# A decoder layer's MLP on Trainium2: conversions and a half block of matmuls issued ahead of other work

## The chip, the cores and the metric

The kernel runs on one core of a Trainium2 chip as a single launch. The metric is the device time of one execution in microseconds. TensorE (PE) does the matrix products, VectorE (DVE), ScalarE (ACT) and GpSimd (POOL) the element-wise work, and SyncE (SP) issues the DMAs. Each engine takes its own instructions in the order in which the program issues them, and engines wait for each other through semaphores; so the order in which the Python program emits instructions is the order within each engine.

## The reference

The reference is one inference step of one decoder layer in float32. It has 512 prompt tokens and 8 samples of 8 tokens, 576 tokens in all, with width 1024. Attention in three dilated groups and a gated linear recurrence run side by side, are gated and merged, projected, added to the input and normalised. The change lies in what follows:

```python
x1 = _layer_norm(DN_ALPHA * x + g1 * mix, ln1_g, ln1_b, dtype)
u2 = x1 * (1 + sc2) + sh2
hid = jnp.square(jax.nn.relu(jnp.einsum('bsd,df->bsf', u2, w_up) + b_up))
ff = jnp.einsum('bsf,fd->bsd', hid, w_down) + b_down
x2 = _layer_norm(DN_ALPHA * x1 + g2 * ff, ln2_g, ln2_b, dtype)
```

The hidden width is 4096. The outputs are both groups' activations, the new caches and the recurrent states.

## The kernel before, in words

**Precision.** Every large product is made of three float32r products. A float32 operand is split into a high part (ACT's copy to float32r: `whi`, `hdh`, `u2h`) and the rest (a subtraction, nearly always on DVE: `wlo`, `hdl`, `u2l`). Then high by high, low by high and high by low are added up in one PSUM bank. So each weight tile costs one ACT and one DVE instruction before PE can use it.

**Weights** come in units of 512 columns, each loaded by SP in two slots of four K tiles (1 MB each). There are three raw buffers (`NRAW = 3`). `load_more` issues the next load when a buffer has been given back by `weights_done`, which is called when the last conversion out of a slot has been issued; the DMA itself then waits for that conversion.

**Order.** The program's main line emits PE's blocks one by one. Side work (the layer norm, transposes, row copies) stands in generators; `side.pump`, called after every few matmuls, advances them by a planner's costs and due times, and `side.drain` runs them out.

**The MLP, from 940 us on.** Tokens are worked on in two halves of 288 (`HF`). The layer norm of half 1 (`layer_norm_1(1)`) runs as side work while the first unit (`mlp[0]`, blocks n = 0 to 3 of the hidden layer, 128 columns each) does half 0. Each half block is 24 matmuls (8 K tiles by 3). `split_once` converts the unit's blocks ahead, the last of them at n = 1. Within the norm, PE sums squares (`sx<-sq`), ACT copies the sum (`lns`), PE spreads it (`sx<-lns`), ACT takes the root and DVE the reciprocal (`lnr`); then come, for each of the 8 K tiles, `u2t`, `u2h` and `u2l`. After `side.drain()` the four blocks of half 1 run interleaved by K tile over four PSUM banks, so that each K tile is used by all four as soon as it is there; then the four evacuations follow (bias and ReLU, square, `hdh`, `hdl`).

After that comes the list `seq` of steps. A `Plain` step is one block of 128 output columns, done as two halves `pe(0)` and `pe(1)`, each followed by its evacuation `ev`. It starts with the second unit (`mlp[1]`, blocks 4 to 7 of the hidden layer) and the first eight blocks of the down product. The other three quarters have up units made of seven block products each (`Seventh`, f = 0 to 6, a Strassen-like scheme with sums of weight blocks and of inputs), two units of 512 columns to a quarter, followed by eight down blocks (`Plain`; only the first two of these three quarters have them in `seq`). The step methods are `sum` (DVE, sums of weight blocks), `cast` (ACT, high part), `low` (DVE, low part), `pe`, `ev`, `fin` (ACT, square and high part of the hidden layer) and `sub` (DVE, its low part). `lag` says how many steps ahead `sum` and `cast` are issued. The loop at the end of the listing writes the order out by hand. Weights of these steps lie in the pool `parts` (6 buffers), which takes the memory of the pools `small` and `caches` that the front part used; `front.close()` gives those back.

**The end.** The last quarter's down product is made in three units `ud[0]`, `ud[1]`, `ud[2]`. `blocks` does the tokens from 256 on, as before with hidden channels on the partitions, and `tokens_major` turns the result by PE transposes (bank `tr`) that ACT and DVE copy out. `tiles` does the first 256 tokens, with tokens on the partitions: per tile of 128 tokens 24 matmuls of 512 columns. The order is `blocks(ud[0])`, `blocks(ud[1])`, `tiles(ud[1])`, `tiles(ud[2])`. `ud[1]` is converted during the fourth block of `ud[0]` (`pass_on`), `ud[2]` during the two tiles of `ud[1]`: K tiles 0 to 3 with the subtraction on POOL, 4 to 7 with it on DVE. `add_up` multiplies a finished tile by the gate (`gps`), adds it to the residual (`res`) and takes statistics (`st`); `normalize` ends the second layer norm with DVE and POOL instructions on `res` and stores the result.

Of the kernel before, what the change touches and what calls it, by code (L numbers as in the profile page):

```python
# [14 lines left out]
AF = mybir.ActivationFunctionType  # L15
# [4 lines left out]
KT = D // 128  # L20
# [5 lines left out]
HF = NT // 2  # L26
# [25 lines left out]
NPG = 62  # L52
NKV = 6
NWP = 6
AHEAD_K = 8
LN2 = 2500
SPH = 0
NRAW = 3
KV_AHEAD = 4
QB_AHEAD = 4  # L60
# [185 lines left out]
def decoder_step(ctx, tc, I, O):  # L246
# [24 lines left out]
    def bank(shape, tag, bufs=2):  # L271
        return psum.tile(shape, F32, name=tag, tag=tag, bufs=bufs)
# [54 lines left out]
    def load_more(force=False):  # L327

        while leaving and (force or leaving[0] <= side.now):
            leaving.popleft()  # L330
        while load_q and live[0] + len(leaving) < NRAW:
            load_one()
# [26 lines left out]
        if j == len(u["blocks"]) - 1:  # L359
            weights_done(u["slots"])  # L360

    def split_k(u, k, eng=V):

        if k in u["w"]:
            return
        load_more(True)
        t = u["slots"][k // 4][2][:, k % 4]
        w = u["w"][k] = page([128, 512], "whi", F32R), page([128, 512], "wlo", F32R)
        A.activation(w[0], t, AF.Copy)
        eng.tensor_sub(w[1], t, w[0])  # L370
        if k % 4 == 3:
            weights_done(u["slots"][k // 4:k // 4 + 1])

    def split_once(u, j):
        if j not in u.setdefault("split", set()):
            u["split"].add(j)
            split(u, j)
# [11 lines left out]
    def mm_part(w, nk, xs, h, ps, ks):  # L389
        hi, lo = w  # L390
        seq = [(hi, 0), (hi, 1), (lo, 0)]
        n = 0
        for k in ks:
            for m, (ww, xi) in enumerate(seq):
                PE.matmul(ps, ww[k // 4][:, k % 4], xs[xi][k][:, h * HF:(h + 1) * HF],
                          start=(k == 0 and m == 0), stop=(k == nk - 1 and m == 2))
                n += 1
                if n % 8 == 0 and n < 3 * len(ks):
                    side.pump(8 * 123.0)
# [1387 lines left out]
    def half(u, j, xs, h, evac):  # L1787
        ps = bank([128, HF], "lin")
        mm_half(u["w"][j], 8, xs, h, ps)
        evac(h, ps)  # L1790
        side.pump(8 * 123.0)
# [3 lines left out]

    u = mlp[0]
    ups = [up_evac(0, n, True) for n in range(4)]
    for n in range(4):
        for m in range(n + 1, min(n + 3, 4)):
            split_once(u, m)  # L1800
        half(u, n, U2, 0, ups[n])
    side.drain()
    banks = [bank([128, HF], "lin" if n < 2 else "att") for n in range(4)]
    for k in range(KT):
        for n in range(4):
            mm_part(u["w"][n], 8, U2, 1, banks[n], (k,))
    for n in range(4):
        ups[n](1, banks[n])
        u["w"].pop(n)

    def down_evac(qd, n):
        def evac(hf, ps):
            if qd == 0:
# [52 lines left out]
    def wpart(shape, name):  # L1866
        return parts["pool"].tile(shape, F32R, name=name, tag="part")
# [16 lines left out]
    class Plain(Step):  # L1884
# [2 lines left out]

        def __init__(self, u, j, xs, evac, order=((0, range(KT)), (1, range(KT)))):
            self.u, self.j, self.xs, self.evac, self.order = u, j, xs, evac, order

        def src(self):
            return [t[:, :, self.j * 128:(self.j + 1) * 128] for _, _, t in self.u["slots"]]
# [16 lines left out]
        def pe(self, i):  # L1909
            h, ks = self.order[i]  # L1910
            self.ps = ps = getattr(self, "ps", {})
            ps[i] = bank([128, HF], "lin")
            for k in ks:
                for m, (w, xi) in enumerate(((self.hi, 0), (self.hi, 1), (self.lo, 0))):
                    PE.matmul(ps[i], w[:, k], hv(self.xs[xi][k], h), start=(k == ks[0] and m == 0),
                              stop=(k == ks[-1] and m == 2))
                if k == ks[3]:
                    side.pump(12 * 133.0)
            side.pump(12 * 133.0)
# [24 lines left out]
    class Seventh(Step):  # L1944


        def __init__(self, unit, f):
            self.U, self.f = unit, f
            self.lag = 2 if f in (1, 2) else 3

        def sum(self):
            f, b = self.f, self.U.blk
# [86 lines left out]
    for qd in range(4):  # L2039
        for n in range(8):  # L2040
            if qd == 0 and n < 4:
                continue
            if qd == 0:
                seq.append(Plain(mlp[1], n % 4, U2, up_evac(0, n)))
            elif n % 4 == 0:
                unit_ = Unit(mlp[qd * 4 + n // 4], qd, n)
                seq += [Seventh(unit_, f) for f in range(7)]
        if qd < 3:
            for n in range(8):

                order = {} if qd == 0 or n else {"order": ((1, (0, 1, 2, 3, 6, 7, 4, 5)), (0, range(KT)))}
                seq.append(Plain(mlp[qd * 4 + 2 + n // 4], n % 4, (Hd[0], Hd[1]), down_evac(qd, n), **order))
# [35 lines left out]
                yield 436, None  # L2088
        gate.append(True)

    front.close()
    parts["pool"] = ctx.enter_context(tc.tile_pool(name="parts", bufs=NWP))
    n_down = len(seq) - 22

    def at(i, what, *a):
        if 0 <= i < len(seq):
            getattr(seq[i], what)(*a)

    at(0, "cast")
    at(0, "low")  # L2100
    for i, st in enumerate(seq):
        if i < 4:
            for k in (2 * i, 2 * i + 1):
                for h in range(2):
                    G.tensor_mul(hv(hT[k], h), hv(hT[k], h), rstds[h])
        if i == 4:
            side.add("p", input_sums())
        if i == 12:
            side.drain()
        if n_down <= i < n_down + 8:  # L2110
            if i == n_down:
                side.flush(True)
                reload(0)
            if i < n_down + 7:
                reload(i - n_down + 1)
        at(i - 1, "ev", 1)
        if i + 1 < len(seq) and seq[i + 1].lag == 1:
            at(i + 1, "cast")
        at(i + 1, "low")
        if i + 2 < len(seq) and seq[i + 2].lag > 2:  # L2120
            at(i + 2, "cast")
        if i and isinstance(st, Plain) and isinstance(seq[i - 1], Seventh):
            for n in (1, 2):
                at(i - n, "fin" if n == 1 else "sub")
            at(i - 1, "sub")
        st.pe(0)
        st.ev(0)
        if not isinstance(st, Plain):
            at(i - 1, "fin")
            at(i - 2, "sub")  # L2130
        if i + 3 < len(seq) and seq[i + 3].lag > 2:
            at(i + 3, "sum")
        if i + 2 < len(seq) and seq[i + 2].lag == 2:
            at(i + 2, "sum")
            at(i + 2, "cast")

        for k in {5: (0, 1), 4: (2, 3), 2: (4, 5), 1: (6, 7)}.get(len(seq) - i, ()):
            split_k(ud[0], k)
        if i >= 6 and i % 2 == 0:
            copy_rows()  # L2140
        st.pe(1)
# [90 lines left out]
    def blocks(w, e):  # L2232
        for n in range(4):
            ps = bank([128, NT - NM], "lin")
            for k in range(KT):
                if n == 0 and k + AHEAD_K < KT:
                    split_k(w, k + AHEAD_K)
                for m, (xi, wi) in enumerate(TERMS):
                    PE.matmul(ps, w["w"][k][wi][:, n * 128:(n + 1) * 128], HD[xi][k][:, NM:NT],
                              start=(k == 0 and m == 0), stop=(k == KT - 1 and m == 2))  # L2240
                if n == 3 and w is ud[0]:
                    pass_on(w, k, ud[1])
                if k % 2 and k < KT - 1:
                    side.pump(6 * 136.0)
            gated(hT[4 * e + n], ps, slice(NM, NT), 5, 4 * e + n)
            side.add("pr"[n % 2], tokens_major(4 * e + n))
            side.pump(6 * 136.0)

    def pass_on(u, k, v):

        if k >= 2:
            u["w"].pop(k - 2)
        if k >= KT - AHEAD_K:
            split_k(v, k - KT + AHEAD_K)

    def tiles(w, e):
        for c in range(NM // 128):
            last = c == NM // 128 - 1

            def before(k):  # L2260
                if w is ud[1]:
                    if last and k >= 2:
                        w["w"].pop(k - 2)
                    if k % 2 == SPH:
                        split_k(ud[2], 4 * c + k // 2, V if c else G)

            for cols in (slice(0, 256), slice(256, 512)) if e and last else (slice(0, 512),):
                ps = mm_tokens(w["w"], HD, lambda t: t[:, c * 128:c * 128 + 128], range(KT), before, cols,
                               "att" if cols.start else "lin")
                add_up(c, e, ps, cols)  # L2270
            if e:
                if last:
                    side.drain()
                moments(c, c + 1)
                normalize(c, last)
# [44 lines left out]
```

## Time and profile before

| what | us |
|---|---|
| time, median of 3 runs | 1382.89 |
| fastest and slowest of them | 1377.75, 1384.52 |
| the profiled execution's own time | 1378.02 |
| its span, first to last instruction | 1376.2 |
| DVE busy | 840.3 |
| ACT busy | 519.9 |
| POOL busy | 324.7 |

The profile is one execution. Its times are microseconds from the start of the span. An idle time stands in brackets with the instruction that ended it, for example "[4.88 <-ACT whi L175]": the engine stood for 4.88 us until ACT had written whi. Nearly all instructions are recorded in one helper (line 175), so they are told apart by engine and tile name. PE's instructions overlap: the duration of one is longer than the distance to the next, so a pace is read from starts, or from counts in a stretch. The MLP takes the part from about 940 us on.

### The profile page before, as it was taken

The page shows a single profiled execution, that of the slowest core. Times are in us where ns is not written, and L with a number is a line of the kernel's source. Part 1 is how long each engine was busy: PE and PEld are TensorE (multiplying, and loading weights), DVE is VectorE, ACT ScalarE, POOL GpSimd, SP SyncE. Part 2 cuts the span into 40 slices and gives each one's busy share as a digit, 9 for nine tenths or more (in the row PEclk, how much of TensorE's full clock was granted, in tenths as well). Part 3 has the DMA queues.
Part 4 walks back from the last instruction along what each step waited for, and adds up shares of the span by engine and source line. Part 5 has one row for each costly group of instructions (what it writes and reads, how often), then busy time and mean ns, then how long its engine had stood idle before and what let it go on. Part 6 is the DMA issues. An engine that isn't in the chain of part 4 may idle for free.

```text
span 1376.2 us, 24394 instructions
## 1 busy us (share of the span) xinstructions
PE 1315.5 (96%) x9480; PEld 1209.6 (88%) x9480; DVE 840.3 (61%) x1674; ACT 519.9 (38%) x1161; POOL 324.7 (24%) x371
## 2 busy tenths in 40 slices
PE   6999999999999999999999999999899999999995
PEld 3889898899878887888989999998899999999994
DVE  2457556558767886666655436547455744756858
ACT  2423333332332222332232442325455732744732
POOL 1232023027417573234343300002410000000005
PEclk9999999999999999999999999999999999999998
DMA  9789899789988977776454313331054433544512
GB/s 306 246 309 323 270 299 355 242 273 324 281 290 286 317 252 242 231 252 200 138 167 141 100 62 123 130 123 62 0 177 153 169 138 117 206 161 154 215 61 69
DMA packets 186824, 274.11 MB, mean 199 GB/s; under 512 B 16012, under 2 KB 92628, under 8 KB 186196
## 3 DMA queue, kind: packets, MB, share of 16 engines
q1 hardware_dynamic: 186708, 272.54, 58.7%
q8 instruction: 75, 1.23, 0.4%
q14 instruction: 41, 0.34, 0.1%
HBM read 212.81 MB, written 76.46 MB: 210 GB/s over the span
## 4 chain that ended last, share of the span: by engine, by line
PE 76%; DVE 10%; DMA 5%; ACT 4%; issue 3%; POOL 1%; SPq 1%; DVEq 0%; POOLq 0%; ACTq 0%
PE lin L175 58%; PE att L175 9%; PE sx L175 6%; DVE wlo L175 4%; PE tr L175 3%; DMA wada<-in_w_ada_dram 2%; DVE res L175 1%; ACT whi L175 1%; ACT sn L175 1%; DMA qb<-qsc 1%; SPq L175 1%; ACT hdh L175 1%; DMA out_dram<-kv 1%; DVE Op L175 1%; DVE hf L175 1%
## 5 line engine op out<-in xcount | busy, mean ns | idle before, releaser
L175 DVE TENSOR_TENSOR wlo<-wraw,whi 128x512 fp32r<-128x512 f32 (+1 forms) x334 | 271.1, 849 | 122.9 <-ACT whi L175 120.0
L175 PE MATMUL lin<-uh,whi 128*128 128x288 f32 x992 | 298.7, 301 | 5.1 <-DVE hso L175 2.4
L175 PE MATMUL lin<-ul,whi 128*128 128x288 f32 x992 | 299.5, 302 | 1.2 <-DVE ul L175 1.2
L175 PE MATMUL lin<-uh,wlo 128*128 128x288 f32 x992 | 298.6, 301 | 1.9 <-DVE wlo L175 1.9
L175 ACT ACTIVATE whi<-wraw 128x512 fp32r<-128x512 f32 (+1 forms) x338 | 211.6, 676 | 118.6 <-PE lin L175 37.0
L175 PEld LDWEIGHTS lin<-ul,whi 128*128 128x128 f32 x992 | 188.0, 189 | 13.8 <-issue 11.0
L175 PEld LDWEIGHTS lin<-uh,whi 128*128 128x128 f32 x992 | 187.8, 189 | 11.3 <-issue 2.9
L175 PEld LDWEIGHTS lin<-uh,wlo 128*128 128x128 f32 x992 | 188.1, 190 | 6.6 <-issue 3.8
L175 POOL TENSOR_TENSOR qb<-qb,kv 128x512 f32<-128x512 f32 x96 | 128.5, 1355 | 203.5 <-PE att L175 65.1
L175 PE MATMUL lin<-hdl,whi 128*128 128x288 f32 (+1 forms) x448 | 133.5, 298 | 4.0 <-DVE hdl L175 4.0
L175 PE MATMUL lin<-hdh,whi 128*128 128x288 f32 (+1 forms) x448 | 134.1, 299 | 0.0
L175 PE MATMUL lin<-hdh,wlo 128*128 128x288 f32 (+1 forms) x448 | 133.2, 297 | 0.0
L175 PEld LDWEIGHTS lin<-hdl,whi 128*128 128x128 f32 x448 | 84.5, 189 | 4.7 <-DVE hdl L175 4.7
L175 POOL TENSOR_TENSOR wlo<-wraw,whi 128x512 fp32r<-128x512 f32 x4 | 6.4, 1603 | 331.5 <-ACT whi L175 331.5
L175 PEld LDWEIGHTS lin<-hdh,whi 128*128 128x128 f32 x448 | 84.5, 189 | 0.0
L175 PEld LDWEIGHTS lin<-hdh,wlo 128*128 128x128 f32 x448 | 84.4, 188 | 0.0
L175 PE MATMUL lin<-whi,uh 128*128 128x512 f32 x160 | 68.4, 428 | 1.3 <-ACT whi L175 1.1
L175 PE MATMUL lin<-wlo,uh 128*128 128x512 f32 x160 | 63.9, 400 | 1.9 <-DVE wlo L175 1.9
L175 DVE TENSOR_REDUCE sc<-qb 128x4 f32<-128x512 f32 x96 | 63.7, 678 | 2.6 <-POOL qb L175 2.4
L175 PE MATMUL lin<-whi,ul 128*128 128x512 f32 x160 | 63.1, 394 | 0.0
L175 PE MATMUL lin<-u2h,whi 128*128 128x288 f32 x176 | 53.0, 301 | 6.1 <-ACT whi L175 4.9
L175 POOL TENSOR_TENSOR hk<-hk,T 128x256 f32<-128x256 f32 (+1 forms) x48 | 40.2, 838 | 72.0 <-PE att L175 43.4
(421 smaller groups left out, 2884.5 us busy)
## 6 DMA issues: line engine op xcount, KB each, us to landing
wraw<-in_w_in_dram SPq DMA_DIRECT2D x42, 1024.0 KB
kv<-in_cache_kv_w_dram SPq DMA_DIRECT2D x144, 256.0 KB
qb<-qsc SPq DMA_DIRECT2D x96, 256.0 KB
wraw<-in_w_down_dram SPq DMA_DIRECT2D x18, 1024.0 KB
out_dram<-kv SPq DMA_DIRECT2D x64, 256.0 KB
wraw<-in_w_ada_dram SPq DMA_DIRECT2D x16, 1024.0 KB
wraw<-in_w_up_dram SPq DMA_DIRECT2D x16, 1024.0 KB
out_dram<-in_cache_kv_w_dram SPq DMA_DIRECT2D x32, 512.0 KB
```

The source lines that it names most:

```text
L175: return f(out, *args, **kw)
```

## The change

Four things are altered.

1. The first half of the second unit's first block (`seq[0].pe(0)` and its evacuation) is issued between `side.drain()` and the interleaved half 1 of the first unit, with a PSUM bank of the tag `tr`. Its conversion (`cast`, `low`) is issued before the first unit's block n = 2, and `front.close()` and the pool `parts` move there with it.
2. At a change from `Seventh` to `Plain` steps, the pending `sub` and `fin` are issued ahead of the next steps' conversions instead of behind them.
3. In the first up unit of a quarter, product f = 2 gets lag 3 instead of 2: its weight sum and its conversion are issued earlier.
4. `ud[2]` is converted during the four blocks of `ud[1]`, two K tiles at a time at k = 2 of each block (the first three pairs by `split_two`, into `parts` buffers, each one ACT and one DVE instruction of double width; the last pair by `split_k`), instead of during the tiles of `ud[1]`. POOL no longer subtracts there.

The constants `AHEAD_K` and `SPH` go; with the value 8 the first never had an effect in `blocks`. The diff, cut to its core:

```diff
-    for n in range(4):
-        for m in range(n + 1, min(n + 3, 4)):
-            split_once(u, m)
-        half(u, n, U2, 0, ups[n])
-    side.drain()
-    banks = [bank([128, HF], "lin" if n < 2 else "att") for n in range(4)]
...
+            self.tags = ("lin", "lin")
...
-            self.lag = 2 if f in (1, 2) else 3
+            self.lag = 2 if f == 1 or f == 2 and not after else 3
...
-                seq += [Seventh(unit_, f) for f in range(7)]
+                seq += [Seventh(unit_, f, n == 0) for f in range(7)]
...
+    for n in range(4):
+        for m in range(n + 1, min(n + 3, 4)):
+            split_once(u, m)
+        if n == 2:
+            front.close()
+            parts["pool"] = ctx.enter_context(tc.tile_pool(name="parts", bufs=NWP))
+            at(0, "cast")
+            at(0, "low")
+        half(u, n, U2, 0, ups[n])
+    side.drain()
+
+    seq[0].tags = ("tr", "lin")
+    seq[0].pe(0)
+    seq[0].ev(0)
+    banks = [bank([128, HF], "lin" if n < 2 else "att") for n in range(4)]
...
         at(i - 1, "ev", 1)
+        if i and isinstance(st, Plain) and isinstance(seq[i - 1], Seventh):
+            at(i - 2, "sub")
+            at(i - 1, "fin")
+            at(i - 1, "sub")
         if i + 1 < len(seq) and seq[i + 1].lag == 1:
             at(i + 1, "cast")
         at(i + 1, "low")
         if i + 2 < len(seq) and seq[i + 2].lag > 2:
             at(i + 2, "cast")
-        if i and isinstance(st, Plain) and isinstance(seq[i - 1], Seventh):
-            for n in (1, 2):
-                at(i - n, "fin" if n == 1 else "sub")
-            at(i - 1, "sub")
-        st.pe(0)
-        st.ev(0)
+        if i:
+            st.pe(0)
+            st.ev(0)
...
-        if i + 3 < len(seq) and seq[i + 3].lag > 2:
-            at(i + 3, "sum")
         if i + 2 < len(seq) and seq[i + 2].lag == 2:
             at(i + 2, "sum")
             at(i + 2, "cast")
+        if i + 3 < len(seq) and seq[i + 3].lag > 2:
+            at(i + 3, "sum")
...
-                if n == 0 and k + AHEAD_K < KT:
-                    split_k(w, k + AHEAD_K)
+                if w is ud[1] and k == 2:
+                    if n < 3:
+                        split_two(ud[2], 2 * n)
+                    else:
+                        split_k(ud[2], 6)
+                        split_k(ud[2], 7)
...
+    def split_two(u, k):
+
+        load_more(True)
+        t = u["slots"][k // 4][2][:, k % 4:k % 4 + 2]
+        hi, lo = (wpart([128, 2, 512], nm) for nm in ("whi", "wlo"))
+        A.activation(hi, t, AF.Copy)
+        V.tensor_sub(lo, t, hi)
+        for i in range(2):
+            u["w"][k + i] = hi[:, i], lo[:, i]
+        if k % 4 == 2:
+            weights_done(u["slots"][k // 4:k // 4 + 1])
...
-                if w is ud[1]:
-                    if last and k >= 2:
-                        w["w"].pop(k - 2)
-                    if k % 2 == SPH:
-                        split_k(ud[2], 4 * c + k // 2, V if c else G)
+                if w is ud[1] and last and k >= 2:
+                    w["w"].pop(k - 2)
```

More of the change, by code (lines that the diff above doesn't have):

```diff
@@ L54 @@
 NWP = 6
-AHEAD_K = 8
 LN2 = 2500
-SPH = 0
 NRAW = 3
@@ L360, in split, with split_k @@
             weights_done(u["slots"])
-    def split_k(u, k, eng=V):
+    def split_k(u, k):
         if k in u["w"]:
@@ L369, in split_k @@
         A.activation(w[0], t, AF.Copy)
-        eng.tensor_sub(w[1], t, w[0])
+        V.tensor_sub(w[1], t, w[0])
         if k % 4 == 3:
@@ L1797, in decoder_step @@
     ups = [up_evac(0, n, True) for n in range(4)]
-    for n in range(4):
-        for m in range(n + 1, min(n + 3, 4)):
-            split_once(u, m)
-        half(u, n, U2, 0, ups[n])
-    side.drain()
-    banks = [bank([128, HF], "lin" if n < 2 else "att") for n in range(4)]
[L1804 to L1809, printed above, removed]
     def down_evac(qd, n):
@@ L1911, in pe @@
             self.ps = ps = getattr(self, "ps", {})
-            ps[i] = bank([128, HF], "lin")
+            ps[i] = bank([128, HF], self.tags[i])
             for k in ks:
@@ L1944, in decoder_step, with __init__ @@
     class Seventh(Step):
-        def __init__(self, unit, f):
+        def __init__(self, unit, f, after):
             self.U, self.f = unit, f
-            self.lag = 2 if f in (1, 2) else 3
+            self.lag = 2 if f == 1 or f == 2 and not after else 3
         def sum(self):
@@ L2089, in residual @@
         gate.append(True)
-    front.close()
-    parts["pool"] = ctx.enter_context(tc.tile_pool(name="parts", bufs=NWP))
     n_down = len(seq) - 22
@@ L2097, in at @@
             getattr(seq[i], what)(*a)
-    at(0, "cast")
-    at(0, "low")
+    for n in range(4):
[12 more added lines that the diff above has]
+    banks = [bank([128, HF], "lin" if n < 2 else "att") for n in range(4)]
+    for k in range(KT):
+        for n in range(4):
+            mm_part(u["w"][n], 8, U2, 1, banks[n], (k,))
+    for n in range(4):
+        ups[n](1, banks[n])
+        u["w"].pop(n)
     for i, st in enumerate(seq):
@@ L2252, in pass_on @@
             u["w"].pop(k - 2)
-        if k >= KT - AHEAD_K:
-            split_k(v, k - KT + AHEAD_K)
+        split_k(v, k)
     def tiles(w, e):
```

## The prediction

> **What bounds the kernel now.** I read the page first, then the busy time by stages, then TensorE's waits in the MLP, and then the timelines of single engines around each wait. From the page:
>
> ```profile
> span 1376.2 us, 24394 instructions
> PE 1315.5 (96%) x9480; PEld 1209.6 (88%) x9480; DVE 840.3 (61%) x1674; ACT 519.9 (38%) x1161; POOL 324.7 (24%) x371
> ```
>
> TensorE (PE) is busy for 96%, so only its idle time can be won by a new order; the diff adds and drops no matmul. The stages of the MLP (columns: stretch, length, busy time of PE, weight loads, VectorE, ScalarE and GpSimd with their instructions, granted clock, DMA share, GB/s):
>
> ```profile
> 940.00:980.00 40.00, 33.01 (x247) 29.64 (x246) 26.02 (x56) 22.97 (x52) 12.49 (x23) 1.00 0.15 53
> 980.00:990.00 10.00, 9.09 (x56) 8.82 (x57) 3.53 (x6) 3.71 (x8) 3.37 (x5) 0.83 0.01 2
> 990.00:1084.00 94.00, 94.00 (x711) 94.00 (x711) 52.58 (x99) 53.96 (x103) 12.33 (x17) 1.00 0.44 160
> ...
> 1340.00:1360.00 20.00, 15.49 (x66) 11.42 (x65) 19.33 (x25) 6.07 (x11) 14.95 (x9) 1.00 0.17 60
> 1360.00:1376.00 16.00, 6.86 (x45) 6.65 (x44) 11.62 (x25) 2.01 (x4) 4.97 (x4) 0.71 0.22 74
> ```
>
> From 990 on PE is saturated: 711 matmuls of 288 columns in 94 us, 0.132 us each. There are holes at both ends: 7 us before 980, and 4.5 us in 1340 to 1360, where VectorE (DVE) is busy for 19.33 of 20 us. After each hole the granted clock is low (0.83 over 10 us, 0.71 over 16 us). Who made PE wait from 940 to the end (total, times, longest):
>
> ```profile
> PE lin L175 <- DVE wlo L175: 5.2, 5, 3.0
> PE lin L175 <- ACT whi L175: 4.9, 1, 4.9
> PE lin L175 <- DVE hdl L175: 4.0, 3, 1.6
> PE lin L175 <- DVE u2l L175: 1.6, 3, 1.0
> PE lin L175 <- ACT u2h L175: 1.2, 1, 1.2
> ...
> PE tr L175 <- ACT res L175: 0.5, 1, 0.5
> ```
>
> Some 17 us in these rows, with the low clock on top. The diff touches three of these places.
>
> **Part 1, the second unit's first block.** Now its conversion (whi, wlo) stands behind the evacuation of the first unit's second token half:
>
> ```profile
> 953.89 0.75 PE L175 MATMUL sx<-lns,comb 128*128 128x288 f32 x2
> ...
> 958.56 0.29 PE L175 MATMUL lin<-u2h,wlo 128*128 128x288 f32 x1
> ...
> 975.58 0.29 PE L175 MATMUL att<-u2h,wlo 128*128 128x288 f32 x1
> 980.75 0.40 PE L175 MATMUL lin<-u2h,whi 128*128 128x288 f32 x1 [4.88 <-ACT whi L175]
> ...
> 989.02 0.29 PE L175 MATMUL lin<-u2h,whi 128*128 128x288 f32 x1
> ```
>
> PE ends that half at 975.7, waits until 980.75, runs the block's 48 matmuls (6.3 us at 0.132) partly at the low clock, and starts the next block at 989.02. The change takes half 0 of this block ahead of the first unit's half 1, with its conversion issued before the first unit's third block (n = 2). Its 24 matmuls (3.2 us) would then fill the wait for the second half of the layer norm, and the hole at 980 would go. But the conversion reads a weight slot whose load starts late (SyncE's queue first, then the DMA traffic by stretches):
>
> ```profile
> 952.51 0.37 SPq L175 DMA_DIRECT2D wraw<-in_w_up_dram  x1
> 953.11 0.37 SPq L175 DMA_DIRECT2D wraw<-in_w_down_dram  x1
> ```
>
> ```profile
> 952.00:953.00 1.00, 1.00 (x18) 0.42 (x11) 1.00 (x2) 0.97 (x3) 0.00 (x0) 1.00 0.00 0
> 953.00:957.00 4.00, 4.00 (x30) 3.82 (x30) 1.86 (x2) 2.52 (x7) 0.80 (x1) 1.00 0.81 262
> 957.00:961.00 4.00, 2.42 (x17) 1.97 (x16) 2.97 (x7) 1.33 (x4) 3.50 (x8) 1.00 0.71 265
> ```
>
> The load at 952.51 is the second slot of the second unit (K tiles 4 to 7): its buffer is free only when the first unit's last block is converted. At 262 GB/s for 4 us, 1.05 MB have moved by 957, which is just this load if the two go in order; if they share, it lands near 960.5. I take 958, a microsecond for the completion (an estimate). [...] Now the queue that the conversion is put into:
>
> ```profile
> 951.07 1.14 ACT L175 ACTIVATE whi<-wraw 128x512 fp32r<-128x512 f32 x2
> ...
> 953.10 0.44 ACT L175 ACTIVATE hdh<-rel 128x288 fp32r<-128x288 f32 x1
> 953.45 0.39 ACT L175 ACTIVATE lns<-sx 128x288 f32<-128x288 f32 x1
> ...
> 974.71 0.50 ACT L175 ACTIVATE rel<-lin,vT 128x288 f32<-128x288 f32 x1 [3.80 <-PE lin L175]
> ...
> 980.08 2.18 ACT L175 ACTIVATE whi<-wraw 128x512 fp32r<-128x512 f32 x4
> ```
>
> The conversion lands on ScalarE (ACT) between the hdh at 953.10 and the lns at 953.45, because the lns is issued inside n = 2, after 8 of its 24 matmuls. Its first instruction (0.55 us) runs at once, its second waits for the load. Queued behind it: lns, then the square root of the norm and the evacuation of n = 2; and PE itself stands at the sx<-lns matmul (953.89), after 16 matmuls of n = 2. So a new wait:
>
> - conversion done at 958.0 + 0.55, lns 0.39 later: PE resumes at 959.0, 5.1 us later than now;
> - that idle time is as long as today's 4.88 us, which was followed by 1.7 us of lost clock (10 us at 0.83). [...] Here the slow stretch may lie partly inside the idle time: 0 to 1.7, I take 0.9;
> - the rest of n = 2 and n = 3 takes 4.8 us now (953.89 to 958.7): until 964.7. Then the new half block, 3.2: until 967.9.
>
> The norm's chain moves with it:
>
> ```profile
> 963.42 0.51 DVE L175 SCALAR_TENSOR_TENSOR u2l<-u2t,b2m,u2h 128x288 fp32r<-128x288 f32 x1
> ...
> 970.37 1.08 DVE L175 SCALAR_TENSOR_TENSOR u2l<-u2t,b2m,u2h 128x288 fp32r<-128x288 f32 x2
> ```
>
> Moved by about 6 us (5.1 and the clock), the second K tile is ready at 969.9 and the last at 977.5; PE asks for the second at 967.9 + 12 x 0.132 = 969.5 and the last at 979. So a wait of 0.4, then 96 matmuls, 12.7: the half ends at 981.0, 5.3 later than now. The block's own half 1 fills until 984.2. The next thing late is the conversion of the block after it, behind the twelve evacuations on ACT: now 980.08, then 985.4, and PE starts 0.67 behind it as today, 986.1, with 0.3 more for wlo. Against 989.02 that is a gain of **2.6 us**. Bounds: 1.0 (all of the clock loss, load shared a little) to 4.5 (load a microsecond earlier, no clock loss). The pools closed earlier cost nothing: no DMA moves at 952 to 953 (0 GB/s), so nobody still reads the memory. The "tr" bank is free there, as no transpose runs between 940 and 980. The POOL products that keep hT now stand behind this block's evacuation, off the path.
>
> **Part 2, the order at changes of stage.** Ahead of the down blocks PE waits once per quarter for hdl:
>
> ```profile
> 1105.19 0.78 ACT L175 ACTIVATE hdh<-sn 128x288 fp32r<-128x288 f32 x2
> ...
> 1106.26 1.14 ACT L175 ACTIVATE whi<-wraw 128x512 fp32r<-128x512 f32 x2
> ```
>
> ```profile
> 1106.91 1.29 DVE L175 TENSOR_TENSOR wlo<-wraw,whi 128x512 fp32r<-128x512 f32 x2 [2.73 <-ACT whi L175]
> 1108.12 1.56 DVE L175 TENSOR_TENSOR hdl<-sn,hdh 128x288 fp32r<-128x288 f32 x4
> ```
>
> The input of the first hdl was there at 1105.97, but DVE, in order, first waited for the whi of the next block and made its wlo. The first hdl is written at 1108.5, and PE asks 1.2 us earlier, at 1107.3. The change issues the two oldest hdl first: 1106.0 to 1106.8. The next block's conversion slips behind the hdh to about 1109.5; PE, with 30 of the present block's 48 matmuls (4.0 us) to go at 1107.3, asks for it at 1111.3. Of the three hdl waits (4.0 us) the two ahead of the down blocks go, 1.2 each; the third (1.6), ahead of the last three units, is not touched. Gain **2.5 us**, between 2.2 and 2.7 (the pipeline's start). The earlier sum and conversion of product 2 in the first unit of a quarter move work that no PE wait shows: 0, hidden by the matmuls of the block before (bounds -0.5 to 0.5). The wlo waits in the quarters' second units ("att", "sx") keep their order and stay.
>
> **Part 3, the last unit's conversion.** Now its eight K tiles are converted during the last token tiles, four of the subtractions by GpSimd (POOL), among the second layer norm:
>
> ```profile
> 1346.96 1.00 DVE L175 TENSOR_TENSOR wlo<-wraw,whi 128x512 fp32r<-128x512 f32 x1
> ...
> 1351.29 3.46 DVE L175 TENSOR_TENSOR wlo<-wraw,whi 128x512 fp32r<-128x512 f32 x2
> 1354.67 3.43 DVE L175 SCALAR_TENSOR_TENSOR res<-res,lnst,lgb 64x512 f32<-64x512 f32 x2
> 1358.03 0.68 DVE L175 TENSOR_TENSOR wlo<-wraw,whi 128x512 fp32r<-128x512 f32 x1
> 1358.63 0.67 DVE L175 TENSOR_TENSOR gps<-lin,gate 128x512 f32<-128x512 f32 x1
> ```
>
> The change does all of it in the four blocks before, where PE is saturated and DVE has room. PE's waits for wlo at the end (most of the 5.2 us) and the low clock behind them go. But PE can't keep all of this: DVE has no gap between these rows, and the sums of finished tiles (gps) queue up behind its norm, so here DVE, not PE, is the end of the chain. What counts is the DVE time that leaves it: 1.00 + 3.46 + 0.68, start to start 4.9 us. POOL's own subtractions go too, and with them some of the slowing (0.68 alone against 1.73 beside POOL), perhaps 1.5 more at best. Against it stands the new place: each pair of tiles is 1.1 us on ACT (the 1.14 above) and 1.3 on DVE (1.29), in the queues that also free the transposes' banks, where PE already waited 0.5 us for ACT res. One such wait grows by about 1.0, the later pairs meet idle stretches. Gain **3.9 us**, between 1.5 (2.4 exposed on top, no change in the slowing) and 6.
>
> **Sum.** 2.6 + 2.5 + 3.9 = 9.0 us. The profiled execution took 1378.02 us (span 1376.2, 1.8 around it), so it would take 1369. It is near the fastest of the three timed runs (1377.75, 1382.89, 1384.52); against their median, 1382.89, I forecast **1373.9 us**. Of this kernel, 0.5% (6.9 us) is about what a measurement can tell from no change.
>
> **Rivals.**
> 1. *The load is there in time, ACT doesn't wait.* Then PE keeps 953.89, runs the new half block at 958.7 to 961.9, the first unit's half 1 to 975.1, and starts the next block at 980.3: part 1 gains 8.7, the sum is 15, 1368. Against it: the load is issued at 952.51, and ACT gets to the second conversion at 954.1.
> 2. *The end gives nothing.* All three pairs hold up PE (3 x 1.3 on DVE) and the norm's own DVE and POOL work fills what wlo leaves. Then 5.1 remain, 1377.8, within 0.5%. For it: DVE was busy 19.33 of 20 us. Against: 5 us of its work really go.
> 3. *Slower: the new wait on ACT is longer.* Each microsecond that the load lands after 958 is one on the path, since lns, PE and the norm all stand behind it. At 967 the gain is used up; at 978 (25 us after issue) the time is 1393.9. Against: both loads, 2.1 MB, had moved by 961.
> 4. *The change doesn't do what it says:* the half block can't start early, as its wlo comes after the norm on DVE. Then part 1 gains nothing or loses 1, about 1377. Against: the subtraction is issued before the norm's reciprocal.
>
> **How the numbers follow.** Forecast 0.72, rival 1 0.08, rival 2 0.11, rival 3 0.04, rival 4 0.05. The forecast's own bounds are 4.7 (1.0 + 2.2 + 1.5) and 13.2 (4.5 + 2.7 + 6), 1369.7 to 1378.2; with rival 1 at the low end, rival 2 at the high end, and a median that can lie some 2 us off, as three runs spread over 6.8, the range is 1366 to 1380. Faster by over 0.5% needs 6.9 us: some nine tenths of the forecast, and rival 1: 0.72. Slower by over 0.5% is rival 3 alone: 0.03. The rest, 0.25, is the same.
>
> **What would show it.** Right: the 4.88 us wait for whi is gone; a new PE wait of about 5 us at sx<-lns near 954, with ACT waiting for the w_up load at its whi; a wait of 1 to 2 us for whi near 984; hdl waits of 1.2 us gone, the one of 1.6 still there; no wlo on DVE or POOL after 1340, and DVE still busy without a gap from the second norm to the end. Wrong: no PE wait near 954 (then rival 1), or PE waiting for "tr" banks or hdl in the last units' blocks by more than 2 us (rival 2).

## The result, and the profile after

The change takes 1372.38 us (median of 8 runs, 1369.33 to 1378.63) against 1381.85 us (8 runs, 1374.66 to 1386.35). The ratio is 0.9943 with a 95% interval of 0.9918 to 0.9967, so 7.9 us faster, between 4.6 and 11.3. The two medians lie 9.5 us apart; all gains in time below go by the ratio, which is taken over all runs. The forecast was 1373.9 us and 9.0 us faster.

The profiled execution has a span of 1371.1 us. The spans of two profiles can't simply be subtracted: the MLP does not begin at the same moment, although the program up to there is the same. The helper that records nearly all instructions stands in line 173 now. The rows of the first u2h matmul (it begins the MLP), of the first matmul of a down block, and of the first token tile, from the view of a tile's instructions; after the count stand minimum, median and maximum duration in ns, then first and last start in us. Before:

```profile
L175 PE MATMUL lin<-u2h,whi x176: 288/295/511, 942.4 to 1280.3; 128*128 128x288 f32 x176
...
L175 PE MATMUL lin<-hdh,whi x448: 293/296/394, 1008.1 to 1336.4; 128*128 128x288 f32 x128, 128*128 128x320 f32 x22
...
L175 PE MATMUL lin<-whi,hdh x32: 282/389/478, 1336.8 to 1363.5; 128*128 128x512 f32 x24, 128*128 128x256 f32 x8
```

And after:

```profile
L173 PE MATMUL lin<-u2h,whi x168: 288/296/511, 945.2 to 1280.6; 128*128 128x288 f32 x168
...
L173 PE MATMUL lin<-hdh,whi x448: 293/296/394, 1011.3 to 1337.5; 128*128 128x288 f32 x128, 128*128 128x320 f32 x22
...
L173 PE MATMUL lin<-whi,hdh x32: 277/389/478, 1337.9 to 1357.2; 128*128 128x512 f32 x24, 128*128 128x256 f32 x8
```

So the front part took 2.8 us longer in this one execution, and the MLP must be counted from its own start. In three stages, with the parts counted as in the prediction (its part 3, the last unit's conversion, is item 4 of the change):

| stage | before | after | difference |
|---|---|---|---|
| A: start of the MLP to the first down block (part 1) | 65.7 | 66.1 | +0.4 |
| B: on to the first token tile (part 2, and the blocks of part 3) | 328.7 | 326.6 | -2.1 |
| C: on to the end of the span (the tiles of part 3) | 39.4 | 33.2 | -6.2 |
| together | 433.9 | 425.9 | -8.0 |

The sum is near the forecast, and its terms are not: nothing came out of part 1, and more out of the end. Who made TensorE (PE) wait in the MLP after the change:

```profile
PE sx L173 <- ACT lns L173: 4.8, 1, 4.8
PE lin L173 <- ACT whi L173: 1.7, 1, 1.7
PE lin L173 <- DVE hdl L173: 1.5, 1, 1.5
PE tr L173 <- ACT res L173: 1.3, 1, 1.3
PE lin L173 <- DVE wlo L173: 0.9, 2, 0.7
```

The 4.9 us wait for whi has become 4.8 us for lns and 1.7 us for whi. Two of the three hdl waits are gone, and so are the wlo waits at the end; the transposes' wait has grown from 0.5 to 1.3. Where the new wait comes from stands in SyncE's queue and in ScalarE's (ACT's) timeline after the change, and what it did to PE in PE's:

```profile
955.37 0.37 SPq L173 DMA_DIRECT2D wraw<-in_w_up_dram  x1
```

```profile
956.31 0.62 ACT L173 ACTIVATE whi<-wraw 128x512 fp32r<-128x512 f32 x1
960.78 0.63 ACT L173 ACTIVATE whi<-wraw 128x512 fp32r<-128x512 f32 x1 [3.85 <-DMA wraw<-in_w_up_dram]
961.31 0.39 ACT L173 ACTIVATE lns<-sx 128x288 f32<-128x288 f32 x1
```

```profile
961.76 1.33 PE L173 MATMUL sx<-lns,comb 128*128 128x288 f32 x2 [4.84 <-ACT lns L173]
...
969.11 0.29 PE L173 MATMUL tr<-u2h,whi 128*128 128x288 f32 x1
...
990.17 0.40 PE L173 MATMUL lin<-u2h,whi 128*128 128x288 f32 x1 [1.74 <-ACT whi L173]
```

The second conversion stands 3.85 us for its load, which was issued 5.4 us before that conversion starts, and the lns behind it, and PE behind that. The half block put ahead (`tr<-u2h,whi`) starts at 969.11 without a wait. The same stretches with the granted clock (the third column from the right):

```profile
957.00:960.50 3.50, 0.00 (x0) 0.00 (x0) 0.83 (x1) 0.00 (x0) 0.28 (x1) 1.00 0.97 347
960.50:967.30 6.80, 5.54 (x21) 5.26 (x22) 3.46 (x4) 2.83 (x6) 0.72 (x1) 0.50 0.32 122
967.30:988.00 20.70, 20.70 (x157) 20.70 (x156) 9.69 (x26) 10.11 (x22) 13.21 (x26) 1.00 0.00 1
988.00:991.20 3.20, 1.27 (x8) 0.80 (x7) 1.97 (x4) 2.96 (x7) 0.10 (x1) 1.00 0.00 0
991.20:994.60 3.40, 3.40 (x16) 3.40 (x15) 2.00 (x4) 1.49 (x3) 0.77 (x1) 0.50 0.01 2
```

The clock is at half for 6.8 us after the first wait and for another 3.4 us after the second, of only 1.7 us. PE works for 5.5 and 3.4 us of this. Its matmuls start 0.241 us apart there (16 steps from 963.12 to 966.97) and 0.132 at the full clock (12 steps from 967.40 to 968.98), so 45% of the 8.9 us is lost: about 4.0 us.

At the end, these rows of VectorE's (DVE's) timeline before stand besides those that the prediction shows:

```profile
1342.10 2.45 DVE L175 SCALAR_TENSOR_TENSOR res<-res,lnst,lgb 128x512 f32<-128x512 f32 x2
...
1347.88 3.48 DVE L175 SCALAR_TENSOR_TENSOR res<-res,lnst,lgb 128x512 f32<-128x512 f32 x2
...
1359.34 0.69 DVE L175 TENSOR_TENSOR res<-res,gps 128x512 f32<-128x512 f32 x1
```

And DVE's and GpSimd's (POOL's) timelines after the change:

```profile
1343.18 1.53 DVE L173 SCALAR_TENSOR_TENSOR res<-res,lnst,lgb 128x512 f32<-128x512 f32 x2
...
1347.12 6.10 DVE L173 SCALAR_TENSOR_TENSOR res<-res,lnst,lgb 128x512 f32<-128x512 f32 x4
1353.15 0.67 DVE L173 TENSOR_TENSOR gps<-lin,gate 128x512 f32<-128x512 f32 x1
1353.86 1.07 DVE L173 TENSOR_TENSOR res<-res,gps 128x512 f32<-128x512 f32 x1
...
1364.49 3.13 DVE L173 SCALAR_TENSOR_TENSOR res<-res,lnst,lgb 128x512 f32<-128x512 f32 x4
```

```profile
1344.31 10.07 POOL L173 TENSOR_TENSOR res<-res,lgb 128x512 f32<-128x512 f32 x6 [331.48 <-ACT res L173]
```

No wlo stands among these any more, on either engine. DVE still works nearly without a gap from 1343 (its longest there is 0.36 us), so it still sets the end.

### The profile page after: what moved, and what is told of

It is laid out like the page before. It is cut to its first block, busy times and chain, and to the rows that moved or that the text cites. A ratio compares the mean times of both kernels' runs of the same rounds, so it can differ in the third digit from the quotient of the medians.

```text
span 1371.1 us, 24387 instructions
## 1 busy us (share of the span) xinstructions
PE 1314.4 (96%) x9480; PEld 1211.3 (88%) x9480; DVE 842.9 (61%) x1675; ACT 520.1 (38%) x1158; POOL 318.6 (23%) x367
## 4 chain that ended last, share of the span: by engine, by line
PE 82%; DVE 8%; ACT 5%; DMA 3%; issue 2%; SPq 0%; POOL 0%; DVEq 0%; POOLq 0%; ACTq 0%
PE lin L173 61%; PE att L173 10%; PE sx L173 7%; PE tr L173 5%; DVE wlo L173 3%; ACT whi L173 1%; DVE res L173 1%; DVE stat_p L173 1%; ACT P L173 1%; DMA qb<-qsc 1%; DMA out_dram<-kv 1%; ACT sn L173 1%; DMA wraw<-in_w_in_dram 1%; DMA xtm<-in_x_prompt_dram 0%; DVE st L173 0%
## 5 line engine op out<-in xcount | busy, mean ns | idle before, releaser
L173 DVE TENSOR_TENSOR wlo<-wraw,whi 128x512 fp32r<-128x512 f32 (+1 forms) x335 | 273.9, 855 | 124.2 <-ACT whi L173 122.4
L173 POOL TENSOR_TENSOR res<-res,lgb 128x512 f32<-128x512 f32 (+2 forms) x10 | 14.8, 1486 | 339.7 <-ACT res L173 339.3
L173 ACT ACTIVATE P<-P,stat_p 128x128 f32<-128x128 f32 (+1 forms) x48 | 20.0, 417 | 99.7 <-DVE stat_p L173 99.7
```

The source lines that it names most:

```text
L173: return f(out, *args, **kw)
```

## The experiments

The theory after reading the two profiles: part 1 is worth about nothing, because the load's wait on ACT and the low clock give back what the filled hole saves; part 2 is worth 2.9 us and part 3 5.5. The rivals: part 1 does bring the gain; the new wait is the norm's own and not the load's; the end is bound by the norm's work and gives little. The ratio is always to the kernel before, run on the same chip as the run: its median there was 1382.90 for e1 to e4, 1380.84 for e5 to e8 and 1379.56 for e9 to e11, so times of different rows are compared by their ratios. Stages A, B and C are read from each run's profile as above. The expectations of e4 and e11 count the four items of the change, not the prediction's parts.

| run | what | time, us (ratio, interval) | A | B | C |
|---|---|---|---|---|---|
| before | | 1381.85 | 65.7 | 328.7 | 39.4 |
| after | the change | 1372.38 (0.9943, 0.9918 to 0.9967) | 66.1 | 326.6 | 33.2 |
| e1 | without part 1 | 1372.99 (0.9926, 0.9905 to 0.9948) | 65.7 | 326.6 | 33.2 |
| e2 | part 1 alone | 1379.54 (0.9980, 0.9964 to 0.9995) | 66.0 | 328.7 | 39.4 |
| e3 | conversion at n = 3 | 1363.89 (0.9860, 0.9838 to 0.9882) | 58.3 | 326.5 | 33.2 |
| e4 | the last unit's move alone | 1374.14 (0.9943, 0.9922 to 0.9965) | 65.8 | 329.6 | 33.2 |
| e5 | load earlier | 1366.31 (0.9881, 0.9856 to 0.9907) | 57.5 | 326.6 | 33.2 |
| e6 | load later | 1375.22 (0.9959, 0.9942 to 0.9976) | 66.4 | 326.6 | 33.2 |
| e7 | e3, next conversion early too | 1364.47 (0.9881, 0.9857 to 0.9904) | 55.8 | 326.6 | 33.2 |
| e8 | e7, last unit's pairs later | 1362.97 (0.9865, 0.9841 to 0.9889) | 55.9 | 325.8 | 33.2 |
| e9 | e5, e7 and e8 together | 1360.79 (0.9856, 0.9837 to 0.9875) | 55.1 | 325.8 | 33.2 |
| e10 | part 2's order alone, one run | 1375.73 | 65.9 | 325.8 | 39.4 |
| e11 | the lag alone, one run | 1378.11 | 66.0 | 328.7 | 39.5 |

In the 13 profiles the MLP begins between 940.7 and 948.2 us, with the same program ahead of it. That spread is nearly as large as the change's whole gain; the stages repeat to some 0.1 us wherever their order is the same, except A (65.7 to 66.0 over before, e1, e4, e10 and e11).

**e1, the change without part 1.**

```diff
-        if n == 2:
-            front.close()
-            parts["pool"] = ctx.enter_context(tc.tile_pool(name="parts", bufs=NWP))
-            at(0, "cast")
-            at(0, "low")
...
-    seq[0].tags = ("tr", "lin")
-    seq[0].pe(0)
-    seq[0].ev(0)
...
+    front.close()
+    parts["pool"] = ctx.enter_context(tc.tile_pool(name="parts", bufs=NWP))
+    at(0, "cast")
+    at(0, "low")
     for i, st in enumerate(seq):
...
-        if i:
-            st.pe(0)
-            st.ev(0)
+        st.pe(0)
+        st.ev(0)
```

> The change without its part 1 (no half block ahead, conversion of the second unit's first block where it was). Theory: part 1 gains between 0 and 2.6 us, because the wait that it adds on ScalarE, with its low clock, eats the hole that it removes. So this kernel is 5.4 to 8 us faster than the kernel before, and its profile has the 4.9 us wait for whi near 980 and no wait at sx<-lns. Rival: part 1 is where the change's gain comes from (its 8.7 us minus little); then this kernel is at most 3 us faster than before.

It is 10.2 us faster than before (7.2 to 13.1), a little more than expected and no less than the change. The rival falls: without part 1 the kernel gains as much. In the trace part 1 costs 0.4 us (A, 66.1 against 65.7).

**e2, part 1 alone.** The edit is the change's first item, on the kernel before.

> Part 1 alone on the kernel before. Theory: 0 to 2.6 us faster, no difference that can be told; a wait of 4.8 us at sx<-lns and 1.7 us for whi in place of 4.9 us for whi. Rival: the wait at sx<-lns is only the norm's idle time shown elsewhere, and the kernel is 6 to 9 us faster.

TensorE's waits in its MLP:

```profile
PE sx L173 <- ACT lns L173: 4.7, 1, 4.7
...
PE lin L173 <- ACT whi L173: 1.7, 1, 1.7
```

2.8 us faster (0.7 to 5.0), a little over the expected range and short of the rival's. The two waits are as expected. Its own profile shows A at 66.0, no gain at all. What makes up the difference between the one profile and the timed runs is not shown.

**e3, the conversion behind lns, the root and the evacuation of n = 2.**

```diff
-        if n == 2:
+        if n == 3:
             front.close()
```

> The change, with the conversion of the second unit's first block issued before the first unit's block n = 3 instead of n = 2, so behind lns, the root and the evacuation of n = 2 on ScalarE. Theory: the load's wait has stood in the norm's way; now ScalarE gets to the conversion about when the load lands, the wait at sx<-lns goes, and the kernel is 6 to 9 us faster than the change (14 to 17 faster than before, about 1366). Rival: the half block put ahead, its bank or the order on TensorE makes the wait; then it takes as long as the change, within 2 us.

ACT's timeline in e3:

```profile
952.14 0.39 ACT L173 ACTIVATE lns<-sx 128x288 f32<-128x288 f32 x1
...
955.79 0.62 ACT L173 ACTIVATE whi<-wraw 128x512 fp32r<-128x512 f32 x1
956.65 0.63 ACT L173 ACTIVATE whi<-wraw 128x512 fp32r<-128x512 f32 x1 [0.23 <-DMA wraw<-in_w_up_dram]
959.01 0.54 ACT L173 ACTIVATE u2h<-u2t,b2m 128x288 fp32r<-128x288 f32 x1 [1.73 <-DVE u2t L173]
```

ACT now waits 0.23 us for the load instead of 3.85, and nothing of the norm stands behind it. A falls to 58.3, 7.8 us less than with the change, as expected; the kernel is 19 us faster than before (16 to 22), more than the 14 to 17 expected. The half block put ahead is still there and in its place, so the rival falls: what cost the time was the place of its conversion.

**e4, the last unit's conversion moved, nothing else.** The edit is the change's fourth item, on the kernel before.

> Part 4 of the change alone (the last unit converted during the blocks before) on the kernel before. Theory from the two profiles: 5.5 us faster (6.2 at the tiles, 0.7 given back by the transposes' wait in the blocks). Rival, the prediction's size: 3.9. Rival 2: the end is bound by the norm's work on VectorE and GpSimd and nothing comes of it, 0 to 1.5.

7.9 us faster (4.8 to 10.8). The trace says 5.3: C falls by 6.2 and B grows by 0.9. Both rivals are too small, by the trace and by the interval, which starts at 4.8; the interval does not tell 5.5 from 7.9.

**e5, the load earlier, the conversion left at n = 2.** The first unit's last block is converted at n = 0. `front.close()`, which e3 moved together with the conversion, stays at n = 2 too.

```diff
-        for m in range(n + 1, min(n + 3, 4)):
+        for m in range(n + 1, 4):
             split_once(u, m)
```

> The change, with the first unit's last block converted at n = 0 instead of n = 1. That gives its raw buffer back earlier, so the load that the new conversion reads is issued some 5 us sooner, while the conversion stays at n = 2. Theory (the load makes the wait): the wait at sx<-lns near 954 goes but for about 1 us that the two extra conversions cost ScalarE, and the kernel is 5 to 8 us faster than the change, 13 to 16 faster than before. Rival (the place in ScalarE's queue costs by itself, whatever the load does): the wait stays at 4 us or more and the time is the change's.

SyncE's queue and ACT's timeline in e5:

```profile
952.50 0.37 SPq L173 DMA_DIRECT2D wraw<-in_w_up_dram  x1
```

```profile
957.72 1.14 ACT L173 ACTIVATE whi<-wraw 128x512 fp32r<-128x512 f32 x2
958.76 0.38 ACT L173 ACTIVATE lns<-sx 128x288 f32<-128x288 f32 x1
```

The load is issued 4.8 us after the start of the MLP (947.7), where the change issues it 10.1 us after (945.2). Both conversions run back to back in front of lns, at the place that the change gave them, and no PE wait for lns is left. A is 57.5, 8.6 us less than with the change; the time is 16 us under that of before (13 to 20). So the late load made the wait; the place in ACT's queue costs nothing when the load is there.

**e6, the load later.** The two loads issued together are swapped.

```diff
+    late = [x for x in load_q if x[0] is mlp[1] and x[1] == 4]
+    at_ = load_q.index(late[0])
+    load_q[at_], load_q[at_ + 1] = load_q[at_ + 1], load_q[at_]
     u = mlp[0]
```

> The change, with the two loads that are issued together swapped, so that the slot which the new conversion reads comes second. Theory, each microsecond that the load is later is one on the path: it lands about 3 us later, the wait at sx<-lns grows from 4.8 to about 8, and the kernel is 2.5 to 4.5 us slower than the change, the clock taking part. Rival: the wait is the norm's own; no difference.

ACT and PE in e6:

```profile
965.64 0.63 ACT L173 ACTIVATE whi<-wraw 128x512 fp32r<-128x512 f32 x1 [6.63 <-DMA wraw<-in_w_up_dram]
```

```profile
PE sx L173 <- ACT lns L173: 7.6, 1, 7.6
```

The wait grew by 2.8 us, as expected, so it is the load's and not the norm's own. The price was not as expected: in the trace A is only 0.3 us longer, so 2.5 us of the longer wait come back elsewhere in A, and where is not shown. In time it is 5.7 us faster than before (3.3 to 8.0) where the change is 7.9 faster; the intervals overlap. So here a microsecond of load is one of waiting (ACT's wait for the load grew from 3.85 to 6.63 us, PE's for lns from 4.84 to 7.6), and its price in time stays open.

**e7, the second block's conversion ahead of the evacuations**, on top of e3.

```diff
     seq[0].ev(0)
+    at(1, "cast")
+    at(1, "low")
...
-        if i + 1 < len(seq) and seq[i + 1].lag == 1:
+        if i and i + 1 < len(seq) and seq[i + 1].lag == 1:
             at(i + 1, "cast")
-        at(i + 1, "low")
+        if i:
+            at(i + 1, "low")
```

> The version with the conversion at n = 3, and besides it the conversion of the second unit's second block issued ahead of the first unit's interleaved half 1, so ahead of the twelve evacuations on ScalarE. Theory: the 1.7 us wait for whi and the 0.2 for wlo behind it go, 2 us faster than the version with n = 3 alone, about 1362, if ScalarE, idle for 5 us there, hides the conversion. Rival: the evacuations, 1.1 us later, hold a bank that the half block behind needs, and as much is given back.

The whi wait is gone, and A falls by 2.5 to 55.8, so the rival falls in the trace. The time, 1364.47, does not show the gain: the intervals of e3 and e7 overlap.

**e8, the last unit's pairs one block later**, on top of e7.

```diff
-                if w is ud[1] and k == 2:
-                    if n < 3:
-                        split_two(ud[2], 2 * n)
-                    else:
-                        split_k(ud[2], 6)
-                        split_k(ud[2], 7)
+                if w is ud[1] and (n, k) in ((1, 2), (2, 2), (2, 6)):
+                    split_two(ud[2], {(1, 2): 0, (2, 2): 2, (2, 6): 4}[n, k])
+                if w is ud[1] and n == 3 and k == 2:
+                    split_k(ud[2], 6)
+                    split_k(ud[2], 7)
```

> The version before this one, and besides it the last unit's first pair of K tiles converted one block later (pairs at the second block, twice at the third, the last at the fourth). Theory: the wait of transposes for ACT res (1.2 us) falls to the 0.5 us that it was before the change, so 0.5 to 1 us faster, about 1361. Rival: two pairs in one block hold up PE there instead; no gain or 1 us slower.

```profile
PE tr L173 <- ACT res L173: 0.5, 1, 0.5
```

The transposes' wait is back at 0.5 us and B falls by 0.8, with C unchanged; by the intervals the time can't be told from e7's.

**e9, all of it.** e8 with the earlier load of e5 and the conversion at n = 2.

> All that gained in the trace: the earlier load with the conversion at n = 2, the second block's conversion ahead of the evacuations, and the last unit's pairs one block later. Theory: 0.5 to 1 us faster than the version with the conversion at n = 3 and the other two, 18 to 20 faster than before, about 1362. Rival: with the load early, the norm's own chain is the bound and nothing more comes; the same time as that version.

A falls by another 0.8, to 55.1. The time is 1360.79, 19.9 us faster than before (17.2 to 22.5), the lowest ratio of all versions; by the intervals it can't be told from e3, e5, e7 and e8.

**e10, part 2's order alone.** The pending sub and fin move ahead of the conversions, as in the change's second item.

> Part 2 alone on the kernel before: the pending sub and fin ahead of the next conversions. Theory, the prediction's 2.5: two hdl waits of 1.2 us go, 1.4 us at each of the two changes from up units to down blocks, and the one of 1.6 stays. Rival: they return as a wait for the next block's whi or wlo.

```profile
PE lin L175 <- DVE hdl L175: 1.6, 1, 1.6
```

B falls by 2.9 us; of three hdl waits one is left, the predicted one, and no new wait has taken their place. It is one run, so only its stages are read.

**e11, the lag alone.** The change's third item.

> Part 3 alone on the kernel before: lag 3 for product 2 of each quarter's first unit. Theory: nothing, within 0.3 us in every stage, and the same waits of TensorE. Rival: the wlo waits of 0.7 us in the quarters' second units go, 2 us.

```profile
PE lin L175 <- DVE hdl L175: 4.0, 3, 1.6
```

B is 328.7 as before and TensorE's waits in it are the same: the lag does nothing here. In the change e4's +0.9 and e10's -2.9 already make up the -2.1 of B to 0.1 us.

## Why the prediction was right or wrong

- **The total was right partly by luck, as its terms' errors cancel.** Forecast 2.6 + 2.5 + 3.9 = 9.0; by the traces -0.4 + 2.9 + 5.4 = 7.9 (8.0 in the table, by rounding); by the runs 7.9. Part 1 came out 3.0 below its forecast, parts 2 and 3 together 1.9 above theirs.
- **Part 1, the mechanism, was right.** The conversion waits on ACT for the load issued when the first unit's last block has been converted; lns and PE stand behind it. The predicted waits were 5.1 us at lns and about 1.7 for whi; measured 4.84 and 1.74. The load was taken to land 5.5 us after its issue (952.51 to 958.0). The conversion starts 5.4 us after the issue (955.37 to 960.78). As for the microsecond for its completion in this: after the change the queues moved 78, 246, 406 and 363 GB/s in the four microseconds from 956.0 to 960.0, 1.09 MB, so if the two loads go in order this load's 1.05 MB had moved by about 959.9, some 0.9 us before the conversion starts (an estimate from these numbers). e5 and e3 show the cause from two sides, and they give nearly what rival 1 had priced at 8.7 us: 8.2 and 7.4 (A against before). So rival 1 was about right in its price and wrong about the change.
- **Part 1, the term that failed: the clock.** The step "0 to 1.7, I take 0.9" counted one stretch of low clock after the long wait, partly hidden. After it came 6.8 us at half clock, and the step at 984 counted none, where the wait of 1.74 us brought another 3.4. No run shows the 0.9; the loss is about 4.0 by the paces measured after the change, 3.1 more. Of this 0.4 came back, since the predicted wait for the norm's second K tile did not come, and another loss of 0.3 is left unexplained. So the gain of 2.6 became a loss of 0.4 in this execution, below the stated bound of 1.0. What part 1 is worth in timed runs stays open: e2 alone gives a gain of 0.7 to 5.0, and e1, which is 10.2 us faster without it where the change is 7.9 faster with it, points the other way.
- **Part 2 was right.** Both 1.2 us waits went and the third stayed; 2.9 against 2.5, a little over the bound of 2.7. With its restart each wait cost 1.5 us: before, PE's starts at the first of them lie at 1107.13, 1108.63 and 1108.87, where the steps are 0.13 otherwise. The lag's 0 was right (e11).
- **Part 3, the right mechanism, was sized too small.** That DVE and not PE sets the end was right: 5.1 us of wlo left its chain. The step took the slowing beside POOL at nothing in its value (1.5 in its bound). In fact, in the rows above, the first pair of the second norm fell from 2.45 us, beside POOL's wlo (two from 1342.37 on, 3.34 us), to 1.53, with POOL idle until 1344.31, and the two pairs behind from 6.91 to 6.10, while one addition slowed from 0.69 to 1.07: 4.9 + 0.9 + 0.8 - 0.4 = 6.2 us. The give-back in the blocks was 0.8 to 0.9 against 1.0, at the predicted place (the transposes' wait, 0.5 to 1.3); e8 gets it back.
- **The rivals.** Rival 2 falls by e4, rival 3 is seen in small in e6 (the longer wait) without its price, rival 4 gives the number that part 1 had in the trace, but not its mechanism: the half block does start early, at 969.11 without a wait, and in e3 it gains 7.4 us.

## What to carry to other kernels

When a step is moved up an in-order queue, look up when each of its inputs lands and what stands behind it in its new place: here the same conversion was worth 7.8 us one block later (e3). Price a TensorE wait with the low clock after it, which may be longer than the wait: 3.4 us after one of 1.74 here. And compare the profiles of two kernels stage by stage from a common event, since the spread of an earlier, unchanged part can hide or feign the gain of the part that was changed.

## What the runs showed of the hardware

Before the change the granted clock stood at half, in the MLP, from 981.11 to 984.52 us, from 1359.99 to 1363.40 and from 1370.23 to the end of the span. After it the clock stood at half from 960.49 to 967.31, from 991.21 to 994.62 and from 1363.26 to the end. So the low stretches that end within the span lasted 3.41 us each, but for one of 6.83, and between the two after the change lie 23.9 us at the full clock.

In the 3.41 us ahead of the four of these stretches that end within the span PE was busy for 0.36 us (977.70 to 981.11) and 1.12 us (1356.58 to 1359.99) before, and for 0.00 us (957.08 to 960.49) and 1.48 us (987.80 to 991.21) after. In the last of these PE waited 1.74 us for whi and 0.19 for wlo (the rows of 988 to 994.6 above). Other waits were followed by no low clock: before, the clock was full from 984.52 to 1359.99, where PE's three hdl waits of 1.2, 1.2 and 1.6 us lie. What makes the difference these profiles do not settle. After the long wait PE was busy for 2.14 of the 3.41 us from 960.49 and for all of the next 3.41, both at half clock, and the clock was full from 967.31; after the second wait it was full again after 3.41 us, in all of which PE was busy.
